# A RetNet and gated-MLP step on one core: the gate's activations in halves, a low part on another engine, and two edits in the retention loop

## The chip, the core and the metric

The kernel runs on one core of a Trainium2 chip, as one program. A core has five engines that work through queues of their own and wait for each other by semaphores: TensorE (PE) for matrix products and transposes, VectorE (DVE) and ScalarE (ACT) for work on tiles, GpSimd (POOL) for tiles and some transfers, and SyncE (SP), which here only issues transfers. Operands lie in the on-chip memory SBUF, products of PE arrive in eight banks of PSUM. The metric is the time of one execution on the device in microseconds.

## What is computed

Two layers over a prompt of 1024 tokens and 8 single new tokens ("decode"), width 1024, all in fp32. The first layer mixes tokens by retention (4 heads, keys of 256, values of 512), the second by a gated MLP whose spatial mixing works on chunks of 128 tokens. The parts of the reference that the change touches:

```python
# retention: o is the retention's output of a head, normalised over its 512 values
mu = jnp.mean(o, -1, keepdims=True)
var = jnp.mean(jnp.square(o - mu), -1, keepdims=True)
o = ((o - mu) * lax.rsqrt(var + LN_EPS)).reshape(B, L, RET_VW) * gn_gain
y = (jax.nn.silu(g) * o) @ w_out
...
# gated MLP
u, v, g = jnp.split(x @ w_in, 3, axis=-1)
u = jax.nn.gelu(u, approximate=False)
v = _layer_norm(jax.nn.gelu(v, approximate=False), ln_g, ln_b)
mixed = jnp.einsum('gij,bcjgd->bcigd', ws, vc) + b_s      # vc: v in chunks of 128 tokens, 8 groups of 256
y = u * mixed * jax.nn.silu(g)
return y @ w_out, v
```

Each layer ends with x = LayerNorm(ALPHA * x + mixer(x)).

## The kernel before

**Products.** An fp32 operand is held as two tiles: a high part `h`, the rounding to a shorter format (fp32r), and a low part `l`, the rest. `mm3` (line 65) makes each product of three matmuls, h·h, h·l and l·h. So whatever goes into PE has to be split first: a copy that rounds (on ACT), and a subtraction for the rest (on DVE or POOL). Some low parts are made in another way: ACT writes -t, rounded, into the low tile (line 1346 for `vl`), and a transfer that POOL issues adds t to it (line 1347), which leaves the rest.

**What sets the order.** The program runs under a manual schedule: every engine executes its instructions in the order in which the Python code emits them. A list `later` collects functions; `run_later` emits what stands in it at the start of the next step. Tiles come from a pool of 49 equal slots, whose reuse makes the writer of a new tile wait for the last reader of the old one; products come in 8 banks of PSUM.

**Retention's chunk loop** (about 581 to 762 us of the span). 16 steps n, four chunks of 256 tokens for each of four heads. In step n the code emits: the statistics of chunk n-1's output (`r_stat`: DVE, then a power on POOL that gives `rs`); for chunk n+1 the transposes of the key `kt`, the split of what was loaded (ACT, then POOL: `qkl`, `vl`), the normalised output of chunk n-1 (`r_on`: `nb` on DVE, then `on` on ACT, line 605) and the scores `sc`; then for chunk n the state update `st`, the inner product and the cross product with the state into `o` (both PE), and the transposes `y` of the normalised chunk n-1 (line 619), which DVE multiplies by the gate into `yT`. The cross product doesn't exist in the first chunk of a head (n%4 = 0).

**The gate stage** (about 1135 to 1540 us). 16 units, two for each of the 8 groups of 256 columns of v; unit n has the tiles fm(40+n). A unit makes 128 columns of u and of s (the gate) at once, with seven products by Strassen-Winograd, in the order p5, p1, p3, p6, p2, p7 and, after the next unit's p5, p4. Each has two steps of 12 matmuls of 258 columns, for the two pieces `c` of half of the tokens. p1, p6, p7 and p4 add up in the same PSUM bank (`fm..a`), p5 and p3 in another (`fm..c`), p2 in a third. After p5, p1 and p3 ACT copies the bank into the tile u or s (line 1189), after p6, p2 and p7 DVE adds it to them (line 1193); p4 ends as a gelu straight from the bank (line 1191). So p6 must wait until ACT has copied, and p7 and p4 until DVE has added. The first half of u, made before, gets its gelu later (line 1200), s its silu (line 1197 in units of odd n, line 1202 in even ones), and then DVE multiplies u and s (line 1203). Beside this, group by group, `s_prep` normalises v (DVE, tiles `lv`) and splits it into `vh` and `vl` and the mixing weight into `wsh` and `wsl`, `s_mix` mixes (PE `mx`, then ACT), and `s_y` transposes the result (PE `yt`, line 1371) and multiplies it by u (DVE `yy`). The weights of the next units are loaded, combined and split in pieces (`wr`, `wt`, `w_p`) in between.

Of the kernel before, what the change touches and what calls it, by code (L numbers as in the profile page):

```python
# [13 lines left out]
AF = mybir.ActivationFunctionType  # L14
ALU = mybir.AluOpType
# [6 lines left out]
T = SEQ + NB  # L22
# [5 lines left out]
NCH = SEQ // CH  # L28
# [6 lines left out]
HT = T // 2  # L35
# [6 lines left out]
def retnet_gmlp_step(ctx: ExitStack, tc: tile.TileContext, a, o):  # L42
    nc = tc.nc
    act, dve, pool, pe, sp = nc.scalar, nc.vector, nc.gpsimd, nc.tensor, nc.sync
# [8 lines left out]
    def S(name, shape=(128, T), dt=F32):  # L53
        return big.tile(list(shape), dt, tag="s", name=name)

    def PS(name):
        return psp.tile([128, 512], F32, tag="ps", name=name)

    def f(ap):
        return ap.bitcast(F32)  # L60
# [4 lines left out]
    def mm3(out, lh, ll, rh, rl, start, stop, skip=False):  # L65
        mm(out, lh, rh, start, False, skip)
        mm(out, lh, rl, False, False, skip)
        mm(out, ll, rh, False, stop, skip)
# [43 lines left out]
    def wload(p):  # L112
        if p >= NP:
            return
        for half in range(2):
            wload_half(p, half)
# [22 lines left out]
    later = []  # L139

    def run_later():
        todo, later[:] = later[:], []
        for fn in todo:
            fn()
# [319 lines left out]
    def dec_gate():  # L464
        dve.tensor_tensor(ydT, ydT, gd, ALU.mult)
        dve.tensor_copy(yd[:, :, 0:8], ydT)
        dve.tensor_tensor(yd[:, :, 8:16], ydT, f(yd[:, :, 0:8]), ALU.subtract)
# [30 lines left out]
    def r_pre(n):  # L498
        if n >= NS:
            r_on(n - 2)  # L500
            return
        r = R[n]
        ps = PS(f"kt{n}")
        for jb in range(2):
            for d in range(2):
                pe.transpose(ps[:, jb * 256 + d * 128:jb * 256 + (d + 1) * 128],
                             r["qk"][:, 2 + d, jb * 128:(jb + 1) * 128], ident)
        kd = S(f"kd{n}", (128, 2, 512), F32R)
        act.copy(kd[:, 0, :], ps)
        dve.tensor_tensor(kd[:, 1, :], ps, f(kd[:, 0, :]), ALU.subtract)  # L510
        r["kd"] = kd
        if n:
            r_split(n + 1)
        r_on(n - 2)
        sc = PS(f"sc{n}")
        hh, ll = r["qkh"], r["qkl"]
        for jb in range(2):
            for d in range(2):
                ks = slice((2 + d) * CH + jb * 128, (2 + d) * CH + (jb + 1) * 128)
                qs = slice(d * CH + jb * 128, (d + 1) * CH)  # L520
                mm3(sc[:, jb * CH:CH + jb * 128], hh[:, ks], ll[:, ks], hh[:, qs], ll[:, qs], d == 0, d == 1)
        pt = S(f"p{n}", (128, 384))
        dve.tensor_tensor(pt, sc[:, :384], RC["mask"], ALU.mult)
        phl = S(f"phl{n}", (128, 2, 384), F32R)
        act.copy(phl[:, 0, :], pt)
        pool.tensor_tensor(phl[:, 1, :], pt, f(phl[:, 0, :]), ALU.subtract)
        r["p"] = phl
# [45 lines left out]
    def r_cross(n):  # L573
        r = R[n]
        if n % NCH == 0:
            return
        sh, sl = r["s"]
        for ib in range(2):
            for d in range(2):
                qs = slice(d * CH + ib * 128, d * CH + (ib + 1) * 128)  # L580
                mm3(r["o"][ib], r["qkh"][:, qs], r["qkl"][:, qs], sh[:, d, :], sl[:, d, :], False, d == 1)

    def r_stat(n):
        if n < 0:
            return
        h, c = divmod(n, NCH)
        r = R[n]
        st = small.tile([128, 2, 6], F32, tag="st", bufs=4, name=f"st{n}")
        mv = small.tile([128, 2, 2], F32, tag="mv", bufs=3, name=f"mv{n}")
        for ib in range(2):  # L590
            dve.bn_stats(st[:, ib, :], r["o"][ib])
        for ib in range(2):
            dve.bn_aggr(mv[:, ib, :], st[:, ib, :])
        r["mv"], r["rs"] = mv, rstd_of(mv[:, :, 1], epsg[:, 2 * h:2 * h + 2], 128, 2, f"n{n}")

    def r_on(n):
        if n < 0:
            return
        r = R[n]
        rs = r["rs"]  # L600
        nb = small.tile([128, 2], F32, tag="nb", name=f"nb{n}")
        dve.scalar_tensor_tensor(nb, r["mv"][:, :, 0], -1.0, rs[:, 0:2], ALU.mult, ALU.mult)
        on = S(f"on{n}", (128, 2, DV))
        for ib in range(2):
            act.activation(on[:, ib, :], r["o"][ib], AF.Identity, bias=nb[:, ib:ib + 1], scale=rs[:, ib:ib + 1])
        r["on"] = on
# [188 lines left out]
    def x_op(key, kt, sl):  # L795

        hh, ll = X[key]
        return hh[kt // 2][:, kt % 2, sl], ll[kt // 2][:, kt % 2, sl]
# [134 lines left out]
    for n in range(NS):  # L933
        run_later()
        if n == 4:
            dec_gate()
        r_stat(n - 1)
        r_pre(n + 1)
        r_state(n)
        r_inner(n)  # L940
        if n % NCH == 1:
            r_cross(n)
        r_y(n - 1)
        if n % NCH != 1:
            r_cross(n)
        r_load(n + 3)
        if n == NS - 5:
            wload(24)
        if n == NS - 4:
            wload(25)  # L950
        if n >= NS - 4:
            wsplit(24, n - NS + 4, eng=pool)
        if n == NS - 1:
            for t2 in range(4):
                outb.ysplit(0, t2)
            outb.pre_load(0)
            outb.pre_load(1)
# [176 lines left out]
    class FmUnit(Unit):  # L1134
# [38 lines left out]
        def step(self, k, c):  # L1173
            ch, first = BANK[k], k in self.FIRST
            if first:
                self.ps[ch, c] = PS(f"fm{self.p}{ch}_{c}")
            ps = self.ps[ch, c][:, :258]
            wh, wl = self.op[k]
            sl = slice(c * 258, c * 258 + 258)
            for kt in range(4):  # L1180
                ws = slice(kt * 128, kt * 128 + 128)
                mm3(ps, wh[:, ws], wl[:, ws], *x_op(XKEY[k], kt, sl), first and kt == 0, kt == 3, skip=not first)
            i, n = OUT[k]
            if k == "p5":
                if c == 0:
                    self.q = [S(f"{s}{self.n}") for s in "us"]
            t = self.q[n][:, i * HT + c * 258:i * HT + c * 258 + 258]
            if k in ("p5", "p1", "p3"):
                act.copy(t, ps)
            elif k == "p4":  # L1190
                act.activation(t, ps, AF.Gelu)
            else:
                dve.tensor_tensor(t, t, ps, ALU.add)
            if c == 1:
                u, s = self.q
                if k == "p7" and self.n % 2:
                    later.append(lambda: act.activation(s, s, AF.Silu))
                if k == "p4":
                    def out():
                        act.activation(u[:, :HT], u[:, :HT], AF.Gelu)  # L1200
                        if self.n % 2 == 0:
                            act.activation(s, s, AF.Silu)
                        later.append(lambda: dve.tensor_tensor(u, u, s, ALU.mult))
                    later.append(out)

    X1_SUMS = {}
    for n, (key, part) in {10: ("s1", 0), 11: ("s1", 3), 13: ("s1", 2), 14: ("s1", 5), 15: ("s2", 0), 16: ("s2", 3),
# [23 lines left out]
    first, at, n = {}, {}, 16  # L1231
# [90 lines left out]
    def s_prep(g, part):  # L1322

        if g >= GR:
            return
        q = G[g]
        if part == 0:
            wr = q["wr"]
            pool.affine_select(out=wr, in_=wr, pattern=[[1, 128]], compare_op=ALU.is_ge, fill=0.0, base=0,
                               channel_multiplier=-1)  # L1330
            wh = small.tile([128, 128], F32R, tag="wsh", name=f"wsh{g}")
            wl = small.tile([128, 128], F32R, tag="wsl", name=f"wsl{g}")
            act.copy(wh, wr)
            dve.tensor_tensor(wl, wr, f(wh), ALU.subtract)
            q["w"] = (wh, wl)
            q["vhl"] = []
        half, k = divmod(part, 4)
        t = q["v"][half]
        tb = half * 4 + k
        dve.scalar_tensor_tensor(t[:, k, :], t[:, k, :], vmv[:, tb, 0:1], q["gt"], ALU.subtract, ALU.mult)  # L1340
        dve.scalar_tensor_tensor(t[:, k, :], t[:, k, :], vrs[:, tb:tb + 1], q["bt"], ALU.mult, ALU.add)
        if k == 3:
            hh = S(f"vh{g}_{half}", (128, 4, 256), F32R)
            ll = S(f"vl{g}_{half}", (128, 4, 256), F32R)
            act.copy(hh, t)
            act.mul(ll, t, -1.0)
            pool.dma_start(ll, t, accum_op=ALU.add)
            q["vhl"].append((hh, ll))

    def s_mix(g):  # L1350
# [102 lines left out]
    for u, k in seq:  # L1453
        for i in range(u.STEPS):
            s = first[u, k] + i
# [95 lines left out]
```

## Time and profile before

| | |
|---|---|
| time, median of 3 runs | 1748.51 us (1746.86 to 1751.27) |
| the profiled execution | 1749.73 us, its span 1748.0 us |
| PE busy | 1692.2 us, 97% of the span |
| DVE busy | 900.0 us, 51% |
| ACT busy | 664.9 us, 38% |
| POOL busy | 407.5 us, 23% |
| granted clock of PE over the span | 0.987 of full speed |

The busy shares are means over stages with different limits. PE's idle time is where another engine sets the pace, and the view of waits tells which; the granted clock is what the throttle gave PE in a stretch, as a share of 2.4 GHz. The profile numbers the units' tiles (fm41a is bank a of the unit with n = 1), but not the chunks: `y` or `on` stand for all.

### The profile page before, as it was taken

How to read it: one execution, taken by the hardware profiler on the slowest of the kernel's cores; microseconds unless marked ns; L12 is line 12 of the kernel's file. 1: busy time of each engine (PE TensorE's matmuls, PEld its weight loads, DVE VectorE, ACT ScalarE, POOL GpSimd, SP SyncE). 2: the span in 40 equal slices, each digit the busy share in tenths (PEclk: the TensorE clock that was granted, in tenths of full speed). 3: DMA queues.
4: the chain of work that ended last, by engine and by line, in shares of the span. 5: the costliest groups of instructions: out<-in, count | busy, mean ns of one | idle time of the engine just before them, and what ended most of it. 6: DMA issues, size and time to landing. Idle time of an engine off the chain costs nothing. (4 is left out here: it accounts for less than half of the span.)

```text
span 1748.0 us, 25438 instructions
## 1 busy us (share of the span) xinstructions
PE 1692.2 (97%) x10304; PEld 1511.5 (86%) x10304; DVE 900.0 (51%) x1446; ACT 664.9 (38%) x1043; POOL 407.5 (23%) x331
## 2 busy tenths in 40 slices
PE   9999999999999999999999999997899999999996
PEld 8898897979999887877778999996889999977775
DVE  7134453633331577753359574564465555543347
ACT  4122424234332454431205343344556666731102
POOL 4122231411110666531107100011111111231103
PEclk9999999999999999999999999998999999999998
DMA  7135555555532544341102312263655666692206
GB/s 266 72 122 191 183 204 187 212 165 209 217 145 93 197 157 157 133 181 49 49 25 110 110 73 97 84 178 78 152 147 151 157 164 157 152 324 89 82 1 171
DMA packets 103174, 248.76 MB, mean 142 GB/s; under 512 B 9264, under 2 KB 37824, under 8 KB 103056
## 3 DMA queue, kind: packets, MB, share of 16 engines
q1 hardware_dynamic: 92736, 222.78, 36.5%
q0 software_dynamic: 10112, 24.15, 7.8%
q8 instruction: 81, 1.33, 0.3%
q14 instruction: 37, 0.30, 0.0%
q10 hardware_dynamic: 208, 0.20, 0.0%
HBM read 152.83 MB, written 69.93 MB: 127 GB/s over the span
## 5 line engine op out<-in xcount | busy, mean ns | idle before, releaser
L63 PE MATMUL fm<-xl,wh 128*128 128x344 f32 x768 | 246.6, 321 | 1.2 <-DVE xl L301 0.8
L63 PE MATMUL fm<-xh,wh 128*128 128x344 f32 x768 | 246.4, 321 | 1.3 <-ACT xh L300 1.3
L63 PE MATMUL fm<-xh,wl 128*128 128x344 f32 x768 | 246.1, 320 | 0.0
L63 PE MATMUL op<-wh,yh 128*128 128x512 f32 x512 | 202.4, 395 | 0.0
L63 PE MATMUL op<-wl,yh 128*128 128x512 f32 x512 | 201.7, 394 | 0.0
L63 PE MATMUL op<-wh,yl 128*128 128x512 f32 x512 | 201.7, 394 | 0.0
L63 PEld LDWEIGHTS fm<-xh,wh 128*128 128x128 f32 x768 | 144.9, 189 | 5.6 <-ACT xh L300 2.0
L63 PEld LDWEIGHTS fm<-xl,wh 128*128 128x128 f32 x768 | 144.7, 188 | 3.0 <-DVE xl L301 1.3
L63 PEld LDWEIGHTS fm<-xh,wl 128*128 128x128 f32 x768 | 144.7, 188 | 0.0
L130 ACT CAST wh<-wr 128x1024 fp32r<-128x1024 f32 x83 | 86.0, 1047 | 143.0 <-PE pd L63 58.9
L665 DVE TENSOR_TENSOR pre<-pre,op 128x512 f32<-128x512 f32 x96 | 65.7, 684 | 141.4 <-PE op L63 141.4
L134 DVE TENSOR_TENSOR wl<-wr,wh 128x1024 fp32r<-128x1024 f32 x77 | 107.6, 1403 | 46.2 <-ACT wh L130 28.6
L412 DVE SCALAR_TENSOR_TENSOR dw<-s,qd_dec,dw 128x512 f32<-128x512 f32 x32 | 40.0, 1251 | 170.1 <-ACT dw L411 170.1
L63 PEld LDWEIGHTS op<-wh,yh 128*128 128x128 f32 x512 | 96.1, 188 | 23.8
L63 PEld LDWEIGHTS op<-wh,yl 128*128 128x128 f32 x512 | 96.1, 188 | 22.7
L63 PEld LDWEIGHTS op<-wl,yh 128*128 128x128 f32 x512 | 96.2, 188 | 22.2
L63 PE MATMUL tm<-wl,xh 128*128 128x512 f32 x256 | 101.1, 395 | 0.0
L63 PE MATMUL tm<-wh,xl 128*128 128x512 f32 x256 | 100.9, 394 | 0.0
L63 PE MATMUL tm<-wh,xh 128*128 128x512 f32 x256 | 100.9, 394 | 0.0
L420 POOL TENSOR_TENSOR dhl<-dw,dhl 128x512 fp32r<-128x512 f32 x32 | 43.3, 1353 | 242.3 <-ACT dhl L419 234.4
L355 ACT ACTIVATE v<-tm,gneg 128x512 f32<-128x512 f32 x32 | 22.0, 689 | 202.3 <-PE tm L63 184.6
L1171 POOL DMA_DIRECT2D w_p<-wr x32 | 28.6, 895 | 295.8 <-PE tm38a L63 169.6
(829 smaller groups left out, 4262.4 us busy)
## 6 DMA issues: line engine op xcount, KB each, us to landing
wr<-in_w SPq DMA_DIRECT2D x127, 512.0 KB
s<-in_state SPq DMA_DIRECT2D x32, 512.0 KB
out_rs<-s SPq DMA_DIRECT2D x32, 512.0 KB
y_s<-yy SPq DMA_DIRECT2D x17, 512.0 KB
qk_s<-ro SPq DMA_DIRECT2D x16, 512.0 KB
v_s<-v SPq DMA_DIRECT2D x16, 512.0 KB
vbc<-vd_s SPq DMA_DIRECT2D x16, 512.0 KB
g_s<-g SPq DMA_DIRECT2D x16, 512.0 KB
```

What stands on the lines that cost most here:

```text
L63: pe.matmul(out, lhs, rhs, start=start, stop=stop, skip_group_check=skip)
L130: act.copy(t, src)
L134: eng.tensor_tensor(t, src, f(W[p][half][0]), ALU.subtract)
L355: act.activation(t[:, i % 2, :], ps, AF.Copy, scale=gneg[:, 2 * h + i % 2:2 * h + i % 2 + 1])
L412: dve.scalar_tensor_tensor(w[:, 0, :], s[:, 0, :], qd_dec[:, h, 0, b:b + 1], w[:, 1, :], ALU.mult, ALU.add)
L420: pool.tensor_tensor(hl[:, 1, :], w, f(hl[:, 0, :]), ALU.subtract)
L665: dve.tensor_tensor(dst, dst, ps, ALU.add)
L1171: pool.dma_start(self.op[k][1], src, accum_op=ALU.add)
```

## The change

Four edits. In retention, `nb` = -mean x rs, one instruction over two columns with two tensor inputs, becomes two instructions over one column, each with one tensor and rs as a scalar operand. The cross product of chunk n is emitted ahead of the transposes of chunk n-1 in all steps; before, only where n%4 was 1. In the gate, silu is cut in two halves of the columns, and the pieces (gelu, silu, silu, product) are emitted one for each step of the schedule in place of together. And `vl` is no longer made by an ACT multiplication and an adding transfer, but by a DVE subtraction that is emitted one step after `vh`.

```diff
         nb = small.tile([128, 2], F32, tag="nb", name=f"nb{n}")
-        dve.scalar_tensor_tensor(nb, r["mv"][:, :, 0], -1.0, rs[:, 0:2], ALU.mult, ALU.mult)
+        for ib in range(2):
+            dve.tensor_scalar(nb[:, ib:ib + 1], r["mv"][:, ib, 0:1], -1.0, rs[:, ib:ib + 1], ALU.mult, ALU.mult)
...
         r_inner(n)
-        if n % NCH == 1:
-            r_cross(n)
+        r_cross(n)
         r_y(n - 1)
-        if n % NCH != 1:
-            r_cross(n)
         r_load(n + 3)
...
                 u, s = self.q
+                lo, hi = slice(0, HT), slice(HT, T)
+                todo = []
                 if k == "p7" and self.n % 2:
-                    later.append(lambda: act.activation(s, s, AF.Silu))
+                    todo = [lambda: act.activation(s[:, lo], s[:, lo], AF.Silu),
+                            lambda: act.activation(s[:, hi], s[:, hi], AF.Silu)]
                 if k == "p4":
-                    def out():
-                        act.activation(u[:, :HT], u[:, :HT], AF.Gelu)
-                        if self.n % 2 == 0:
-                            act.activation(s, s, AF.Silu)
-                        later.append(lambda: dve.tensor_tensor(u, u, s, ALU.mult))
-                    later.append(out)
+                    todo = [lambda: act.activation(u[:, lo], u[:, lo], AF.Gelu)]
+                    if self.n % 2 == 0:
+                        todo += [lambda: act.activation(s[:, lo], s[:, lo], AF.Silu),
+                                 lambda: act.activation(s[:, hi], s[:, hi], AF.Silu)]
+                    todo.append(lambda: dve.tensor_tensor(u, u, s, ALU.mult))
+
+                def chain():
+                    if todo:
+                        todo.pop(0)()
+                        later.append(chain)
+                later.append(chain)
...
             act.copy(hh, t)
-            act.mul(ll, t, -1.0)
-            pool.dma_start(ll, t, accum_op=ALU.add)
+            later.append(lambda: dve.tensor_tensor(ll, t, f(hh), ALU.subtract))
             q["vhl"].append((hh, ll))
```

How the order of the engines moves, at three places. The rows name line, operation and out<-in; a number right behind a name is the chunk, group or unit. The lines of the changed kernel are numbered by its own code.

PE in step n = 6 of the retention loop, where the inner product of chunk 6 (o6 from vh6, vl6) is followed by the transposes of chunk 5 and the cross product of chunk 6 (o6 from sh5, sl5). Before:

```order
L63 MATMUL o6_1_5545<-vl6_5281,phl6_5406 128x512
L63 MATMUL o6_1_5545<-vh6_5280,phl6_5406 128x512
L619 MATMUL y5_0_5556<-ident_71,on5_5502 128x128 x4
L619 MATMUL y5_1_5563<-ident_71,on5_5502 128x128 x4
L63 MATMUL o6_0_5544<-sh5_5426,qkh6_5276 128x512
L63 MATMUL o6_0_5544<-sl5_5427,qkh6_5276 128x512
```

Now, from the last cross products on:

```order
L63 MATMUL o6_1_5551<-sh5_5431,qkh6_5279 128x512
L63 MATMUL o6_1_5551<-sl5_5432,qkh6_5279 128x512
L63 MATMUL o6_1_5551<-sh5_5431,qkl6_5280 128x512
L620 MATMUL y5_0_5574<-ident_71,on5_5508 128x128 x4
L620 MATMUL y5_1_5581<-ident_71,on5_5508 128x128 x4
L506 MATMUL kt8_5604<-ident_71,qk8_5473 128x128 x4
```

The two groups of four transposes moved behind all 12 matmuls of the cross product, up to the transposes `kt` of the next step.

ACT between unit 10 (tiles fm50, u10, s10) and unit 11 (fm51), behind unit 10's last product. Before:

```order
L1191 ACTIVATE u10_12867<-fm50a_0_12918 128x258
L1191 ACTIVATE u10_12867<-fm50a_1_12933 128x258
L1200 ACTIVATE u10_12867<-u10_12867 128x516
L1202 ACT_TABLE_LOAD
L1202 ACTIVATE s10_12868<-s10_12868 128x1032
L1333 CAST wsh6_13200<-gbw6_13112 128x128
L1189 COPY u11_13129<-fm51a_0_13206 128x258
L1189 COPY u11_13129<-fm51a_1_13221 128x258
```

Now:

```order
L1189 ACTIVATE u10_12881<-fm50a_0_12933 128x258
L1189 ACTIVATE u10_12881<-fm50a_1_12948 128x258
L1200 ACTIVATE u10_12881<-u10_12881 128x516
L1339 CAST wsh6_13213<-gbw6_13126 128x128
L1187 COPY u11_13143<-fm51a_0_13219 128x258
L1202 ACT_TABLE_LOAD
L1202 ACTIVATE s10_12882<-s10_12882 128x516
L1187 COPY u11_13143<-fm51a_1_13234 128x258
L1203 ACTIVATE s10_12882<-s10_12882 128x516
```

The copy of the mixing weight `wsh6` moved from behind the silu to ahead of the table load, and the two copies of unit 11's bank now stand ahead of and between the two halves of the silu.

DVE in unit 11, from the last normalisation of the first half of group 6's v (lv6_0) on. Before:

```order
L1341 SCALAR_TENSOR_TENSOR lv6_0_13108<-lv6_0_13108,vrs_105,gbw6_13112 128x256
L1193 TENSOR_TENSOR u11_13129<-u11_13129,fm51b_0_13332 128x258
L1036 TENSOR_TENSOR w52_p1_13323<-wr52_0_13071,w52_p1_13323 128x512
L1193 TENSOR_TENSOR u11_13129<-u11_13129,fm51b_1_13347 128x258
L1193 TENSOR_TENSOR s11_13130<-s11_13130,fm51a_0_13206 128x258
L1193 TENSOR_TENSOR s11_13130<-s11_13130,fm51a_1_13221 128x258
```

Now:

```order
L1347 SCALAR_TENSOR_TENSOR lv6_0_13122<-lv6_0_13122,vrs_105,gbw6_13126 128x256
L1191 TENSOR_TENSOR u11_13143<-u11_13143,fm51b_0_13345 128x258
L1352 TENSOR_TENSOR vl6_0_13343<-lv6_0_13122,vh6_0_13342 128x1024
L1034 TENSOR_TENSOR w52_p1_13338<-wr52_0_13085,w52_p1_13338 128x512
L1191 TENSOR_TENSOR u11_13143<-u11_13143,fm51b_1_13361 128x258
L1191 TENSOR_TENSOR s11_13144<-s11_13144,fm51a_0_13219 128x258
L1191 TENSOR_TENSOR s11_13144<-s11_13144,fm51a_1_13234 128x258
```

The subtraction for vl6_0, which reads ACT's vh6_0, stands ahead of a weight piece, the second add into u11 and the adds into s11 of product p7.

## Rows read from the trace of the kernel before

**Rows 1.** Waits of PE, by releaser: us in total, times, longest us.

```profile
PE y L619 <- ACT on L605: 10.3, 12, 2.4
PE mx L63 <- DMA vl<-lv: 7.9, 2, 4.7
PE yt L1371 <- ACT u L1191: 3.9, 2, 3.1
...
PE fm44c L63 <- ACT s L1189: 2.3, 1, 2.3
PE fm41a L63 <- ACT u L1189: 2.0, 1, 2.0
...
PE fm43a L63 <- DVE s L1193: 1.2, 1, 1.2
```

**Rows 2.** Busy us by stretch: length, engines, PE clock, DMA share, GB/s.

```profile
600.00:700.00 100.00, 91.30 (x488) 75.94 (x487) 77.03 (x139) 49.62 (x66) 61.79 (x38) 0.97 0.44 145
1150.00:1300.00 150.00, 128.94 (x935) 122.48 (x936) 77.21 (x162) 75.28 (x137) 21.11 (x26) 0.92 0.52 125
1300.00:1510.00 210.00, 208.55 (x1696) 205.92 (x1695) 133.08 (x279) 131.54 (x238) 35.04 (x43) 1.00 0.63 158
```

**Rows 3.** The instructions of line 602: duration ns min/median/max, first and last start.

```profile
L602 DVE SCALAR_TENSOR_TENSOR nb<-mv,rsrn x16: 160/2331/2391, 596.6 to 757.9; 128x2 f32<-128x2 f32 x16
```

**Rows 4.** Timeline around chunk 1's `on`: start us, us, instruction, [idle before, releaser].

```profile
604.07 0.40 PE L63 MATMUL st<-vl,kd 128*128 128x512 f32 x1
...
604.30 0.63 PE L63 MATMUL st<-vh,kd 128*128 128x512 f32 x2
...
607.28 2.38 POOL L495 TENSOR_TENSOR qkl<-qk,qkh 128x1024 fp32r<-128x1024 f32 x1
...
607.34 2.33 DVE L602 SCALAR_TENSOR_TENSOR nb<-mv,rsrn 128x2 f32<-128x2 f32 x1 [0.20 <-POOL rsrn L254]
...
610.60 0.33 PE L619 MATMUL y<-ident,on 128*128 128x128 f32 x1 [2.42 <-ACT on L605]
```

**Rows 5.** Timeline of POOL and DVE at two later places of the span.

```profile
939.28 2.39 POOL L713 TENSOR_TENSOR pred<-pred,lnb 8x1024 f32<-8x1024 f32 x1
...
939.77 0.15 DVE L251 TENSOR_SCALAR rstl<-lmv 128x1 f32<-128x1 f32 x1
...
1526.53 4.78 POOL L134 TENSOR_TENSOR wl<-wr,wh 128x1024 fp32r<-128x1024 f32 x2 [11.02 <-ACT wh L130]
...
1529.01 2.33 DVE L1380 CAST y1d<-ydt 128x8 fp32r<-128x8 f32 x1
```

**Rows 6.** The tile vl: time from a transfer's issue to its landing.

```profile
DMA to landing us min/median/max: 4.5/6.1/8.8
```

**Rows 7.** DVE's subtraction of 128x1024 on line 1036: duration ns min/median/max.

```profile
L1036 DVE TENSOR_TENSOR wl_p<-wt,wh_p x6: 1218/1222/1227, 1010.8 to 1121.1; 128x1024 fp32r<-128x1024 f32 x6
```

**Rows 8.** Timeline of ACT in the gate stage, units 41 and 44.

```profile
1212.57 1.06 ACT L1346 ACTIVATE vl<-lv 128x1024 fp32r<-128x1024 f32 x1 [0.64 <-DMA w_p<-wt]
...
1266.73 0.62 ACT L1164 CAST w_p<-wr 128x512 fp32r<-128x512 f32 x1 [5.22 <-DMA vl<-lv]
```

**Rows 9.** Timeline of ACT, DVE and PE in unit 51.

```profile
1443.93 1.05 ACT L1345 CAST vh<-lv 128x1024 fp32r<-128x1024 f32 x1 [0.96 <-PE fm51a L63]
...
1444.10 0.68 DVE L1036 TENSOR_TENSOR w_p<-wr,w_p 128x512 fp32r<-128x512 f32 x1
...
1445.04 0.75 DVE L1193 TENSOR_TENSOR s<-s,fm51a 128x258 f32<-128x258 f32 x2
...
1447.92 0.28 PE L63 MATMUL fm51a<-x1h,w_p 128*128 128x258 f32 x1
```

**Rows 10.** Timeline of ACT and DVE between units 50 and 51.

```profile
1430.56 1.28 ACT L1202 ACT_TABLE_LOAD   x1
...
1432.83 0.28 ACT L1333 CAST wsh<-gbw 128x128 fp32r<-128x128 f32 x1
...
1433.14 0.29 DVE L1334 TENSOR_TENSOR wsl<-gbw,wsh 128x128 fp32r<-128x128 f32 x1 [9.55 <-ACT wsh L1333]
```

## The prediction

> **What bounds the kernel now.** TensorE (PE) is busy nearly throughout, as the table of the profile says, and the change leaves its matmuls and transposes as they are. So it can win only PE's idle time and the time that PE runs at a lower clock. The first view is who waited for whom on PE [rows 1]: the reader is to see that the largest waits stand in the two stages that the change touches. In the chunk loop of retention the transposes `y` wait 10.3 us for `on`, in 12 places. In the gate stage `mx` waits 7.9 us for the transfer that makes `vl`, `yt` 3.9 us for a gelu, fm44c 2.3, fm41a 2.0 and fm43a 1.2 us for copies and adds on ScalarE (ACT) and VectorE (DVE). The second view, busy time and granted clock by stretch [rows 2], adds what waits cost behind themselves. From 600 to 700 PE is idle for 8.7 us and its granted clock averages 0.97 of 2.4 GHz; from 1150 to 1300 it is idle for 21.1 us at 0.92; from 1300 to 1510 it is idle for 1.5 us at 1.00. Busy time at a lower clock loses the missing share: 0.03 x 91.3 = 2.7 us in the loop, 0.08 x 128.9 = 10.3 us in the gate. So one us of wait costs (8.7 + 2.7) / 8.7 = 1.31 us in retention and (21.1 + 10.3) / 21.1 = 1.49 us in the gate's first part. With 10.3 x 1.31 = 13.5 us in retention and 31.4 in the gate, 45 us is all there is to win; the forecast is what part of it goes.
>
> **Retention, the mean term.** `nb` takes between 160 and 2391 ns, with a median of 2331 [rows 3]. The timeline shows why: one starts at 607.34 and ends at 609.67, just when the subtraction for `qkl` on GpSimd (POOL, 607.28 to 609.66) ends; ACT's `on` has to wait for it, and PE has idled 2.42 us for `on` at 610.60 [rows 4]. This DVE instruction with two tensors from SBUF stands still beside POOL's. The change replaces it with two instructions of one column that read one tensor each. The trace has such a one: `rstl`, one column, one tensor, took 0.15 us at 939.77 although a sum on POOL ran from 939.28 to 941.67. It also has a row against it: the cast of `y1d`, 8 columns and one tensor, took 2.33 us from 1529.01, and ended at 1531.34, just when two subtractions on POOL, one after the other from 1526.53, ended at 1531.31 [rows 5]. So the bounds for the pair are 0.30 and about 2.4 us. I take 0.30, because `rstl` is the same operation in the same shape. The Trainium skill ("SBUF — State Buffer", section "Who interferes with whom") says that a VectorE instruction with one SBUF input keeps clear of GpSimd outside the two-port modes, but that a tensor_scalar can enter such a mode and then contends. The `y1d` row agrees with the second half, the `rstl` row with the first; by the second half alone, rival (a) below would come out.
>
> **Retention, the order.** In the iterations with n%4 of 2 and 3 (8 of 16), the 12 matmuls of the cross product now stand ahead of the 8 transposes of y; with n%4 = 1 they did already, with n%4 = 0 there is no cross product. Matmuls of this width follow each other by 0.23 us (604.07 and 604.30 [rows 4]), so `on` gets 12 x 0.23 = 2.8 us more, and the longest wait for it was 2.4 [rows 1]. No transfer moves with it. The price: DVE's statistics of the next chunk now stand behind its evacuation of the later y, so `nb` and `on` of that chunk come later against PE. Where the next iteration has a cross product, that hides it; in n = 4, 8 and 12 nothing does, and I allow 0.15 us each at 1.31, which with rounding is 0.5 us. So of the 13.5 us **13.0** go. The two edits cover each other: for all but the chunks in front of n = 4, 8 and 12 either would do.
>
> **Gate, the low part of v.** It was an ACT multiplication, a DMA issued by POOL, and a landing 4.5 to 8.8 us after the issue, with 6.1 as the median [rows 6]. Now DVE subtracts, 128x1024 from two SBUF tensors: 1.22 us by `wl_p`, the same form [rows 7]. ACT loses 16 x 1.06 us [rows 8], POOL 16 issues, DVE gains 16 x 1.22 = 19.5 us. In the steady part DVE is busy for 133.1 of 210 us [rows 2], so the sum has room; the question is only what stands behind it. The two `mx` waits go, since the subtraction takes the place of a multiplication and of at least 4.5 us to the landing: 7.9 x 1.49 = **11.8**. The fm44c wait goes too: ACT's cast at 1266.73 had idled for 5.22 us until a `vl` transfer landed, and the copy that PE waited for stood behind it [rows 8]. I take **3.0** of 2.3 x 1.49 = 3.4.
>
> A new wait comes with it: the subtraction waits for ACT's vh, and queued behind it on DVE are a weight piece and the adds into u and s, for which PE's next product waits. In unit 51 vh ran from 1443.93 to 1444.98; a weight piece and an add began at 1444.10 and took until the s adds at 1445.04, of which two last 0.75 us; and PE began the product p4, which needs the first, at 1447.92 [rows 9]. With the subtraction in front, the first s add ends at 1444.98 + 1.22 + 0.94 + 0.38 = 1447.52 (half of the two adds), 0.40 us before PE needs it. So it costs nothing there, but only just. At the gate's start (units 40 to 44) the slots of the pool come free in another order, and I expect DVE to hold up a copy for product p6 of unit 41 in place of ACT: **-2.0** there, an estimate that takes fm41a's 2.0 us once more. Bounds: +3.0 if fm41a's wait goes (2.0 x 1.49), -7.2 if four of the first five units wait the 1.2 us of a subtraction.
>
> **Gate, halves.** The silu over 1032 columns becomes two pieces; the gelu stays one piece of 516, and a step of the schedule lies between pieces. The number of table loads stays. ACT's `wsh` came at 1432.83, behind the table load that began at 1430.56 and the whole silu; DVE's queue idled for 9.55 us until it, and began at 1433.14 [rows 10]. Now `wsh` stands right behind the gelu, where the load stood: 1432.83 - 1430.56 = 2.27 us earlier, and the whole run of DVE's work behind it too. That removes fm43a's wait, 1.2 x 1.49 = **1.8**; in the steady part there is no PE wait to remove. For `yt`, the multiplication of 1.06 us and the 0.64 us idle ahead of it, between the two gelus [rows 8], leave the path: 1.7 x 1.49 = **2.5**; vh stays between them, and with it the rest of that wait. The product u*s of even units (about the 1.22 us of [rows 7]) moves from ahead of two weight pieces to right ahead of the yy product that reads it. That costs nothing while the 2.27 us earlier start hides the wait for the second silu half; without it, 1.2 us in each even unit's successor.
>
> **The sum.** 13.0 + 11.8 + 3.0 + 1.8 + 2.5 - 2.0 = 30.1 us. The profiled execution took 1749.7 us, 1.7 more than its span, and the median of the three runs was 1748.5. The profiled execution is 1.2 us off that median, so the terms are taken over unscaled: 1748.5 - 30.1 = **1718 us**.
>
> **Rivals.** (a) *The pair waits for POOL like the old instruction.* For it: the `y1d` cast; against it: `rstl` [rows 5]. The reordering still covers the chunks that are followed by a cross product, but the three y in n = 4, 8 and 12, whose statistics come later into POOL's run, pay 2.2 us each: 3 x 2.2 x 1.31 = 8.6, which gives 1727. (b) *The gate's start trades one wait for another.* DVE waits for vh, a slot or the decode rows ahead of the adds in units 41 to 45; the lower bound comes, 5.2 us worse, and yt's 2.5 stay: 1726. (c) *DVE's queue becomes the bound*, slower than before. If vh comes later than now, each odd unit's s adds come later by as much. Up to 0.40 us that is free; at 4 us the eight odd units pay 8 x 3.60 x 1.49 = 43 us, which gives 1761. For it: that margin. Against it: ACT has 16 x 1.06 us less to do. It crosses the old time at about 30.1 / (8 x 1.49) + 0.40 = 2.9 us of lateness. (d) *The waits only change owner* in both stages, and PE waits as long for another releaser: 1747.
>
> **How the numbers follow.** The forecast has 0.70, (a) 0.10, (b) 0.13, (c) 0.04, (d) 0.03. The forecast's own spread is 1709 to 1725: below, 3.0 in place of -2.0 and the rest of `yt` (2.2 x 1.49 = 3.3); above, half of the mx gain lost. The range goes on to 1732 over (a) and (b) and what they share, and down to 1706 for small waits that I left out. Faster by over 0.3% (about 5 us, what a measurement of this kernel can tell from no change) holds the forecast, (a) and (b): 0.93; within it (d): 0.03; slower (c): 0.04.
>
> **What would show it.** In the changed kernel's trace: 32 instructions of `nb` near 0.15 us with POOL running beside them; no `y` wait above 0.4 us, and a clock of 1.00 from 600 to 700; no wait of `mx`; a DVE `vl` of 1.22 us; `wsh` ahead of the table load and DVE's run some 2.3 us earlier; units 45 to 54 without PE waits. It would be wrong if `nb` still takes 2.3 us, if products p4 or p7 of odd units wait for s adds, or if units 41 to 43 still show several us of waits.

## The result, and the profile after

| | before | after |
|---|---|---|
| median | 1748.34 us (4 runs) | 1729.13 us (4 runs, 1728.48 to 1731.05) |
| ratio | | 0.989, 95% interval 0.9873 to 0.9907 |
| profiled execution, its span | 1749.73, 1748.0 us | 1728.71, 1726.9 us |

The kernel became faster by 19.2 us, 1.1%. The forecast was 30.1 us less, 1718; the time lies inside the range of 1706 to 1732, near its upper end. The direction and most of the mechanisms held, and a third of the forecast gain is missing. The rest of this document is about that third.

The view of PE's waits of the changed kernel, with the columns of [rows 1]:

```profile
PE fm41c L63 <- ACT s L1187: 4.4, 2, 3.9
PE fm42a L63 <- DVE s L1191: 3.0, 2, 2.4
PE fm41a L63 <- ACT u L1187: 3.0, 1, 3.0
PE op L63 <- DVE yl L643: 2.9, 1, 2.9
PE yt L1376 <- ACT u L1189: 2.8, 2, 1.5
PE fm41a L63 <- DVE s L1191: 2.7, 1, 2.7
...
PE fm55a L63 <- DVE s L1191: 1.5, 1, 1.5
...
PE y L620 <- ACT on L606: 0.7, 2, 0.3
...
PE fm43a L63 <- DVE s L1191: 0.6, 1, 0.6
```

Against [rows 1], the 10.3 us of `y` became 0.7, `mx` and fm44c no longer wait for a transfer or a copy, fm43a's wait halved. New at the top are three waits of unit 41, one of unit 42 and one of `op`, the first product behind the retention loop. Busy time and clock by stretch, to be laid beside [rows 2] (the gate's stretches begin 11 us earlier here, as the gate does):

```profile
600.00:700.00 100.00, 99.29 (x556) 84.57 (x555) 77.17 (x163) 53.52 (x70) 73.95 (x42) 1.00 0.44 147
1139.00:1289.00 150.00, 131.76 (x996) 126.71 (x997) 92.94 (x185) 73.36 (x143) 16.68 (x21) 0.94 0.41 109
1289.00:1500.00 211.00, 211.00 (x1713) 208.35 (x1713) 137.80 (x273) 126.59 (x242) 26.22 (x33) 1.00 0.53 139
```

In the loop PE is now idle for 0.7 of 100 us at a full clock, in place of 8.7 at 0.97. In the gate's first part it is still idle for 18.2 us, where it was 21.1: that is where the forecast's gain is missing.

Where the time went is read from when a tile's first matmul starts (the number behind the min/median/max). Before, then after:

```profile
L63 PE MATMUL op<-wh,yh x512: 387/394/482, 751.6 to 1733.8; 128*128 128x512 f32 x171
...
L63 PE MATMUL fm40c<-xs1h,w_p x16: 278/284/289, 1135.3 to 1138.1; 128*128 128x258 f32 x16
L63 PE MATMUL fm42c<-xs1h,w_p x16: 277/416/419, 1195.0 to 1199.3; 128*128 128x258 f32 x16
L63 PE MATMUL fm46c<-xs1h,w_p x16: 278/283/289, 1310.1 to 1312.8; 128*128 128x258 f32 x16
```

```profile
L63 PE MATMUL op<-wh,yh x512: 387/394/484, 736.7 to 1712.5; 128*128 128x512 f32 x171
...
L63 PE MATMUL fm40c<-xs1h,w_p x16: 278/282/287, 1124.0 to 1126.7; 128*128 128x258 f32 x16
L63 PE MATMUL fm42c<-xs1h,w_p x16: 277/282/286, 1188.4 to 1191.2; 128*128 128x258 f32 x16
L63 PE MATMUL fm46c<-xs1h,w_p x16: 277/282/293, 1290.0 to 1292.8; 128*128 128x258 f32 x16
```

The out-projection of retention (`op`) begins 14.9 us earlier; at the gate's begin (fm40c), behind the new wait of `op`, 11.3 of that are left. From there to unit 42 the changed kernel *loses* 4.7 us (6.6 left at fm42c), although the first wait of mx, 4.7 us, lay in that stretch and is gone; from unit 42 to unit 46 it wins 13.5 (20.1 at fm46c). Behind that little changes: the span ends 21.1 us earlier. (Both profiled executions stand within 1.5 us of their medians, so this differs a little from 19.2.)

More than half of what was won from unit 42 to 46 is clock, not waits. PE's busy time and granted clock from fm40c to fm42c and from there to fm46c (stretch, length, PE busy, clock, DMA share, GB/s), before, then after:

```profile
1135.30:1195.00 59.70, 51.17 (x383) 0.94 0.65 164
1195.00:1310.10 115.10, 100.99 (x746) 0.93 0.50 125
```

```profile
1124.00:1188.40 64.40, 53.76 (x382) 0.87 0.47 122
1188.40:1290.00 101.60, 93.49 (x745) 1.00 0.46 127
```

From fm40c to fm42c PE's idle time grew from 8.5 to 10.6 us, and its busy time by 2.6 us at a lower clock. From fm42c to fm46c the idle time fell from 14.1 to 8.1 us and the busy time by 7.5, because the clock was 1.00 in place of 0.93.

### The profile page after: what moved, and what is told of

Read it like the earlier page. It is cut to its first block, busy times and chain, and to the rows that moved or that the text cites. A ratio compares the mean times of both kernels' runs of the same rounds, so it can differ in the third digit from the quotient of the medians.

```text
span 1726.9 us, 25389 instructions
## 1 busy us (share of the span) xinstructions
PE 1682.3 (97%) x10304; PEld 1507.2 (87%) x10304; DVE 907.9 (53%) x1478; ACT 655.4 (38%) x1045; POOL 399.0 (23%) x315
```

## The experiments

**The four parts alone.** First, only the mean term:

```diff
-        dve.scalar_tensor_tensor(nb, r["mv"][:, :, 0], -1.0, rs[:, 0:2], ALU.mult, ALU.mult)
+        for ib in range(2):
+            dve.tensor_scalar(nb[:, ib:ib + 1], r["mv"][:, ib, 0:1], -1.0, rs[:, ib:ib + 1], ALU.mult, ALU.mult)
```

> Only the mean term: two one-column instructions in place of one. Theory: either retention edit alone covers most of the waits of the transposes. nb then takes about 0.21 us each of two beside GpSimd as in the changed kernel, on comes 1.9 us earlier in the nine chunks that had a slow nb, so the four long waits of y (1.3 to 2.4 us) shrink under 0.5 us, 10.3 us of waits become 3 and the time falls by 9 to 12 us, to about 1738. Rival: the order is what did it, and the time falls by less than 4 us.

Measured: 1736.06 us against 1748.92, ratio 0.9924 (0.9906 to 0.9942), 12.9 us less. The instructions of nb in this kernel (ns min/median/max), and its wait of y:

```profile
L603 DVE TENSOR_SCALAR nb<-mv,rsrn x32: 203/210/220, 596.3 to 744.9; 128x1 f32<-128x1 f32 x32
...
PE y L620 <- ACT on L606: 1.5, 5, 0.3
```

None of the 32 is over 0.22 us, though a POOL subtraction ran beside 22 of them, where nine of the 16 old ones stood near 2.35 beside POOL. That settles the mean term: it alone brings what I had forecast for both retention edits (13.0), and a little more than the 9 to 12 us expected of it here.

Second, only the order:

```diff
-        if n % NCH == 1:
-            r_cross(n)
+        r_cross(n)
         r_y(n - 1)
-        if n % NCH != 1:
-            r_cross(n)
```

> Only the order: the cross product ahead of the transposes in all steps, nb as before. Theory: the chunks that are followed by a cross product are covered, as with the mean term alone (9 us less), but some of the three transposes in steps 4, 8 and 12 get a slow nb, 2.2 us each with nothing to cover it, so the fall is 4 to 9 us, to about 1742. Rival: the order does everything by itself, 13 us less; then the mean term is worth nothing.

Measured: 1751.64 us, ratio 1.0014 (1.0004 to 1.0024), 2.7 us *more*, where I had expected 4 to 9 less. The other eight waits of y are 0.34 us or less, so the cover works for PE there; but `op` waits 0.9 and 0.8 us, which it did not before, and the three waits in steps 4, 8 and 12 came (2.45, 2.29 and 2.91 us). My reason for those was wrong. The timeline of this kernel around step 4, all engines:

```profile
618.03 2.35 DVE L602 SCALAR_TENSOR_TENSOR nb<-mv,rsrn 128x2 f32<-128x2 f32 x1 [0.27 <-POOL rsrn L254]
...
620.41 1.45 ACT L605 ACTIVATE on<-o,nb,rsrn 128x512 f32<-128x512 f32 x2 [5.29 <-DVE nb L602]
...
622.16 1.07 ACT L559 ACTIVATE so<-T 128x1024 f32<-128x1024 f32 x1
...
623.25 0.40 SPq L560 DMA_DIRECT2D out_rp<-so  x1
623.75 0.53 SPq L482 DMA_DIRECT2D qk<-qk_s  x1
...
627.43 0.16 DVE L602 SCALAR_TENSOR_TENSOR nb<-mv,rsrn 128x2 f32<-128x2 f32 x1 [0.27 <-POOL rsrn L254]
...
628.41 1.05 ACT L494 CAST qkh<-qk 128x1024 fp32r<-128x1024 f32 x1 [4.45 <-DMA qk<-qk_s]
...
631.21 1.44 ACT L605 ACTIVATE on<-o,nb,rsrn 128x512 f32<-128x512 f32 x2
...
632.03 0.33 PE L619 MATMUL y<-ident,on 128*128 128x128 f32 x1 [2.45 <-ACT on L605]
```

The nb of the chunk that waits (627.43) is short. It is the one *before* it that is slow (618.03): it holds up `on`, behind which ACT makes the head's state `so`, for which the store `out_rp` waits in SP's queue, and behind the store the loads of a later chunk. ACT idles 4.45 us for that load, and `on` stands behind the split of what is loaded. So PE, ahead by what the order won, meets loads that come no earlier. A further kernel tested this: as the one just shown, with the store emitted a step later, behind the loads:

```diff
-            sp.dma_start(o["rp"][h].rearrange("(d p) e -> p d e", p=128), so)
+            later.append(lambda: sp.dma_start(o["rp"][h].rearrange("(d p) e -> p d e", p=128), so))
```

> As e2_order (the cross product first, nb as before), and the store of a head's state (out_rp from so) is emitted one step later, behind the three loads of the chunk that is fetched three steps ahead. Theory: in e2_order the y of steps 4, 8 and 12 waited because SyncE's queue held the loads of qk behind that store, which waits for so, which ACT executes behind the on that a slow nb holds up; with the store behind the loads, ACT no longer idles 4 to 5 us for qk there, the waits of 2.4, 2.3 and 2.9 us shrink below 1 us, and the time falls by 6 to 10 us against e2_order, to about 1743. Rival: the loads wait for their own slots or for the memory, and come no earlier: 1751.

Measured: 1742.22 us, ratio 0.996 (0.9945 to 0.9975), 9.4 us below the order alone. What ACT idled for `qk` on line 494 (us, times), with the order alone and then with the store moved, and the remaining wait of y in the second:

```profile
  DMA qk<-qk_s: 17.4, 5
```

```profile
  DMA qk<-qk_s: 2.6, 2
...
PE y L619 <- ACT on L605: 4.9, 15, 1.1
```

With the store behind the loads, most of ACT's idle time for `qk` is gone, and so are the long waits of y. That shows the chain: a slow nb holds up ACT, ACT the store, and the store the loads behind it in SP's queue. The nb of step 4 is now itself slow, as the prediction had feared (2.34 us at 627.52), but y waits only 1.07 us there.

Third, only the halves (the part of the diff in `step` that builds `todo` and `chain`):

```diff
-                    later.append(lambda: act.activation(s, s, AF.Silu))
+                    todo = [lambda: act.activation(s[:, lo], s[:, lo], AF.Silu),
+                            lambda: act.activation(s[:, hi], s[:, hi], AF.Silu)]
...
-                    def out():
...
+                    todo = [lambda: act.activation(u[:, lo], u[:, lo], AF.Gelu)]
...
+                    todo.append(lambda: dve.tensor_tensor(u, u, s, ALU.mult))
```

> Only the halves of silu and their spread over steps; the low part of v as before. Theory: the mixing weight's copy comes 2.3 us earlier, the waits of fm43a and fm45a (2.6 us) go, the two waits of mx for the transfer stay, so 2 to 5 us less, about 1745. Rival: the pieces shift the slots of the pool and cost at the gate's start what the changed kernel lost there in unit 41 (7 us of waits, some 10 in time), so 5 us more than before, about 1753.

Measured: 1751.01 us, ratio 1.0009 (0.9998 to 1.002): no difference that can be told. Both theories missed. fm43a no longer waits (1.2 us before), and `mx` waits 6.3 us in place of 7.9, but fm45a's wait stayed (1.6 us), and the trace has new waits for s adds (fm41a 2.7 us where the kernel before had 1.1 in all, fm53a 1.6 where there was none).

Fourth, only the low part of v:

```diff
-            act.mul(ll, t, -1.0)
-            pool.dma_start(ll, t, accum_op=ALU.add)
+            later.append(lambda: dve.tensor_tensor(ll, t, f(hh), ALU.subtract))
```

> Only the low part of v by a VectorE subtraction. Theory: the mx waits and fm44c's go (15 us), and the subtraction, which waits for the slot of a weight piece that product p3 of unit 41 reads, holds up the decode rows and the copies behind them there: waits of 4, 3 and 3 us at fm41c and fm41a, which cost 10 us; so 5 us less, about 1743. Rival: the hold-up in unit 41 comes from the halves, and this part alone gives the 15 us, about 1733.

Measured: 1738.63 us, ratio 0.9941 (0.9921 to 0.9962), 10.3 us less, between the theory's 5 and the rival's 15. Its waits of PE show what it costs:

```profile
PE fm41c L63 <- ACT s L1189: 4.4, 2, 3.8
PE fm41a L63 <- ACT u L1189: 3.0, 1, 3.0
```

So this part, and not the halves, makes these two waits of unit 41. The four differences add up to -12.9 + 2.7 + 2.1 - 10.3 = -18.4 us, near the -19.2 of all four together.

**Parts taken back from the changed kernel.** The old order of the loop in an otherwise changed kernel:

```diff
-        r_cross(n)
+        if n % NCH == 1:
+            r_cross(n)
         r_y(n - 1)
+        if n % NCH != 1:
+            r_cross(n)
```

> The changed kernel with the retention loop's old order; the other three parts stay. Theory: with the short nb the order saves only some waits of 0.1 to 0.3 us, 1.2 us in all, and costs 3 us at the loop's end, where the first product of the out-projection waits 2.9 us for a subtraction on VectorE that stands beside GpSimd's. Undoing it gives 2 us, to about 1727. Rival: the order is worth its part of what I forecast, and undoing it costs 2 us or more, 1731.

Measured: 1726.42 us, ratio 0.9864 (0.985 to 0.9879), 2.7 below the changed kernel. The interval still touches that of the changed kernel, so the size is not sharp; but op no longer waits in its trace. The old order in the last step alone:

```diff
-        r_cross(n)
+        if n < NS - 1:
+            r_cross(n)
         r_y(n - 1)
+        if n == NS - 1:
+            r_cross(n)
```

> The changed kernel with the old order in the last step of the retention loop alone (transposes of chunk 14 ahead of the cross product of chunk 15). Theory: there the later transposes make VectorE's first subtraction for the out-projection start behind GpSimd's, where it stands still; with the old order in this step alone the wait of 2.9 us at op goes and the time falls by 2 to 4 us, to about 1726. Rival: the wait has to do with the short nb, not the order, and stays: 1729.

Measured: 1726.52 us, ratio 0.9867 (0.9853 to 0.9882), the same again. DVE's and POOL's timeline at the loop's end, in the changed kernel (with PE's wait) and then with the old last step:

```profile
736.76 5.74 POOL L643 TENSOR_TENSOR yl<-yT,yh 128x1024 fp32r<-128x1024 f32 x2 [2.25 <-ACT yh L642]
...
738.12 5.46 DVE L643 TENSOR_TENSOR yl<-yT,yh 128x1024 fp32r<-128x1024 f32 x2
...
740.31 0.50 PE L63 MATMUL op<-wh,yl 128*128 128x512 f32 x1 [2.90 <-DVE yl L643]
```

```profile
736.17 1.22 DVE L643 TENSOR_TENSOR yl<-yT,yh 128x1024 fp32r<-128x1024 f32 x1
...
736.87 6.16 POOL L643 TENSOR_TENSOR yl<-yT,yh 128x1024 fp32r<-128x1024 f32 x2 [2.28 <-ACT yh L642]
```

The subtraction yl for the out-projection has two tensors from SBUF. Behind the later transposes DVE begins its first at 738.12, when POOL has been at its own for 1.4 us, and stands still for a while; with the old last step it begins 0.7 us ahead of POOL's and takes 1.22 us.

The silu in one piece in an otherwise changed kernel (the old lines of `step`, as in the diff above, with plus and minus exchanged):

> The changed kernel with silu in one piece and emitted as before; the other three parts stay. Theory: the halves put the product of u and s of even units among the adds that p7 waits for, which cost 1.6 us more in unit 41 and 1.4 more in unit 42, and save 0.7 in unit 43 and 0.5 in unit 55; undoing them gives 2 to 3 us, to about 1726.5. Rival: they give the 1.8 us forecast, and undoing costs that, 1731.

Measured: 1730.95 us, ratio 0.9891 (0.9876 to 0.9907), against 0.989 (0.9873 to 0.9907) with the halves: not told apart. In its trace the s waits of fm41a fall from 2.7 to 1.0 us, as I had expected, but that of fm42a only from 3.0 to 2.8, and those of fm43a and fm55a rise from 0.6 to 1.3 and from 1.5 to 2.0. The halves shift waits; neither my +1.8 nor the loss that I then expected is shown.

**The gate's start.** The changed kernel's timeline in unit 41, ACT, DVE and PE:

```profile
1161.63 1.04 ACT L1351 CAST vh<-lv 128x1024 fp32r<-128x1024 f32 x1 [3.72 <-issue]
1162.58 0.37 ACT L1187 COPY s<-fm41c 128x258 f32<-128x258 f32 x1
...
1163.00 0.58 PE L63 MATMUL fm41c<-xs4h,w_p 128*128 128x258 f32 x1 [3.85 <-ACT s L1187]
...
1166.04 1.22 DVE L1352 TENSOR_TENSOR vl<-lv,vh 128x1024 fp32r<-128x1024 f32 x1 [12.60 <-PE fm41c L63]
1167.18 1.27 DVE L1293 SCALAR_TENSOR_TENSOR vd<-vd,vdmv,vdg 8x1024 f32<-8x1024 f32 x1
...
1168.48 0.38 ACT L1187 COPY u<-fm41a 128x258 f32<-128x258 f32 x1 [4.45 <-DVE vd L1293]
...
1168.91 0.58 PE L63 MATMUL fm41a<-xs2h,w_p 128*128 128x258 f32 x1 [2.96 <-ACT u L1187]
```

DVE's queue stands for 12.60 us at the first vl. It does not wait for vh, which is there at 1162.67, but until PE ends product p3 (fm41c), which makes nothing that vl reads: it is the last reader of the tile in whose slot vl is put (w41_p3, weights of p3). PE for its part ran p3 late, because the copy of s stands on ACT behind vh, and vh had waited for its slot (the profile names no releaser; in the program the slot held wt41_1, which is read by a transfer that POOL issued at 1158.21 and that landed 3.3 us later). Behind vl on DVE is vd, the normalisation of the decode rows; the copy of u waits for vd, because it takes the slot of what vd reads (vdg0). So p6 waits too. The next kernel takes vd out of that queue by emitting it two steps earlier:

```diff
-        if (fb, o) in ((1, 2), (4, 2)):
+        if (fb, o) in ((1, 0), (4, 2)):
             vd_norm(fb // 4)
```

> The changed kernel with the normalisation of the decode rows (vd) emitted two steps earlier, ahead of the subtraction for the first vl in place of behind it. Theory: the waits of 3.9 us at fm41c and 3.0 at fm41a come from slots of the pool that are let go too late because the subtraction holds up the queue of VectorE; with vd ahead, the subtraction's slot and that of vh come free by the end of p1, the two waits shrink to under 2 us together, and the time falls by 5 to 9 us, to about 1722. Rival: the vd rows must wait for their own loads there, the waits only move, and the time stays at 1729.

Measured: 1718.7 us, ratio 0.9821 (0.9804 to 0.9837), 10.4 below the changed kernel. That is a little more than expected. Both waits are gone from the view of waits; vl on DVE and the gate's first part (the columns of [rows 2]):

```profile
1159.53 1.23 DVE L1352 TENSOR_TENSOR vl<-lv,vh 128x1024 fp32r<-128x1024 f32 x1 [1.12 <-ACT vh L1351]
...
1139.00:1289.00 150.00, 139.65 (x1089) 134.99 (x1088) 102.07 (x208) 81.25 (x158) 18.49 (x23) 0.98 0.46 124
```

vl now waits 1.12 us, for vh. PE's idle time there falls from 18.2 to 10.4 us and its clock rises from 0.94 to 0.98. In the program the edit does two things: it takes vd out of the queue behind vl, and, since vd's tiles come free earlier, it deals out the slots anew. The first vl now stands in the slot of w41_p1, whose last reader is the earlier product p1, and vh in that of vd itself. That fits the slots as the cause; the two effects, and the single slots, were not tried apart.

**Better versions.** Both repairs together, the early decode rows and the old last step:

> The changed kernel with both repairs: the decode rows normalised two steps earlier, and the old order in the last step of the retention loop. Theory: the two lie in different stages and add up, 10.4 + 2.6 us less than the changed kernel's 1729.1, so 1716. Rival: they share something (the out-projection's start moves what arrives at the gate's start), and the sum is 1718 to 1719.

Measured: 1714.34 us, ratio 0.9807 (0.9794 to 0.9821): the lowest median here. At 14.8 us below the changed kernel, the two add up or a little more. Last, the same with vh a step later, to take it from between the gelus that yt waits for:

```diff
-            act.copy(hh, t)
-            later.append(lambda: dve.tensor_tensor(ll, t, f(hh), ALU.subtract))
+            def split():
+                act.copy(hh, t)
+                later.append(lambda: dve.tensor_tensor(ll, t, f(hh), ALU.subtract))
+            later.append(split)
```

> As f1_both, and the copy vh is emitted one step later, so that it no longer stands between the two gelus that the yt transposes of unit 41 wait for. Theory: the second wait of yt shrinks from 1.5 to under 0.5 us, which is worth 1.5 us, so 1714.5; the subtraction, one more step behind, still comes before mx. Rival: vh comes later, so DVE's queue waits longer for it ahead of the s adds, and units 42 and later wait for those: 1718 or more.

Measured: 1716.18 us, ratio 0.9813 (0.98 to 0.9826), not told apart from the last one. Its waits show the exchange: yt's second wait is gone, and unit 42's wait for s, 1.6 us in the kernel with both repairs, more than doubled.

```profile
PE fm42a L63 <- DVE s L1194: 3.5, 1, 3.5
...
PE yt L1382 <- ACT u L1192: 1.3, 1, 1.3
```

```profile
1188.56 1.29 DVE L1385 TENSOR_TENSOR yy<-yt,u 128x512 f32<-128x512 f32 x2 [9.58 <-DMA w_p<-wt]
```

The later vh is not what holds up the adds: vl has no wait in this run of DVE's work. The run begins with yy, behind a transfer, and goes on with hardly a stop to the s add that PE waits for, at 1198.69, some 10 us later. In the kernel with both repairs it is as long (1189.33 to 1199.46; there it begins with vl, which had waited for vh). So a PE that comes earlier to unit 42 only waits longer. DVE's queue is the bound there, as in rival (c) of the prediction, but not for the reason (c) gives.

## Why the prediction held, and where it missed

**What bounds the kernel** was right: nearly all that was won was PE's idle time and clock in the two stages, and the part behind unit 46 gave only 1.0 us. The price of 1.31 to 1.49 us for each us of wait held as a mean over the gate's first part: in the changed kernel 18.2 us of idle time stand beside 0.06 x 131.8 = 7.9 us lost to the clock, a price of 1.43, and with the early decode rows 10.4 beside 2.8, a price of 1.27. It is not the price of a single wait. From fm42c to fm46c the changed kernel was idle for 8.1 us at a clock of 1.00. And behind the same 2.9 us of `op`, the clock was 1.00 in the changed kernel (741 to 744) and 0.50, the lower level of 1.2 GHz, in the one with the early rows (740.95 to 744.20).

By the starts of the tiles, retention and what follows it up to the gate won 11.3 us of the 13.0 forecast, and the gate up to unit 46 won 8.8 (20.1 less 11.3) of 17.1. So most of what is missing lies in the gate.

**The mean term** was right in mechanism and size: 0.21 us for each of 32, and 0.33 for a pair, whose second begins before the first has ended, against the 0.30 taken from `rstl`; the loop won 14.1 us up to `op` (14.9 less the 0.8 by which it began earlier), 13.0 with the mean term alone. Rival (a) is refuted by the row of nb above. The Trainium skill ("SBUF — State Buffer", section "Who interferes with whom") says that a tensor_scalar can enter a two-port mode, and then contend with GpSimd, where its operands meet that mode's conditions. The 0.20 to 0.22 us of nb beside POOL show no such contention for one column. The same section of the Trainium skill says that a VectorE instruction with two SBUF inputs contends with a GpSimd instruction that reads SBUF. The `yl` rows above agree (2.13 us for the first behind POOL's, 1.22 ahead of it).

**The order** was sized too well. Three things failed. "Either would do" for all but three chunks: alone, the order lost 2.7 us, since the slow nb acts through the store and the loads as well, which I had not followed. "No transfer moves with it": true of the emission, but the queue of SP waits for ACT, and that I had left out. And the price at the loop's end was missing: I priced the later transposes only by the next step's nb and on, and the last step has no next one; behind it stand the subtractions for the out-projection, beside POOL. That was 2.9 us of wait, some 2.6 in time.

**The low part of v** brought in sum what was forecast where it should, but in part by luck. mx's 7.9 us and fm44c's 2.3 are gone, and from unit 42 to 46 the kernel won 13.5 us; the forecast's terms for that stretch are the second mx wait (3.2 x 1.49 = 4.8), 3.0, 1.8 and 2.5, together 12.1. The items differ. The 1.4 us of fm45a, which also went, I had left out, and fm42a waits 2.4 us longer for s. PE's idle time fell by only 6.0 us in all; the other 7.5 are clock, where the price of 1.49 would give 2.9. The tight place in unit 51 held: no unit from 45 to 54 waits.

**The term that was mis-sized is the gate's start**, -2.0 with a lower bound of -7.2. From fm40c to fm42c the kernel lost 4.7 us net of the first mx wait. With that wait at its bare 4.7 us, the price was 9.4 us; at the forecast's 4.7 x 1.49 = 7.0 it was 11.7. It lies between, since a part of the clock that the old wait cost fell behind fm42c, whose matmuls took 416 ns before and take 282 now. The end of the chain, which I had named (DVE holds up a copy for p6 of unit 41), was there and cost 2.96 us of wait. What I did not see was its start: that vl's slot hangs on p3, and that vh waits for a slot too, with the copy of s behind it on ACT (3.85 us); and u*s in the run of adds made p7's wait 2.7 in place of 1.1. My bound assumed that each unit would at most wait for one subtraction of 1.2 us; the queue waited 12.60 us for a slot. This one term explains 7.4 to 9.7 of the 10.9 us between forecast and result, and `op` some 2.6. Taking back `op`'s wait and two of unit 41's three gave 1714.

**The halves** were forecast at 1.8 + part of the yt term. wsh did come earlier and fm43a's wait halved, but runs with and without them can't be told apart. The sentence "That costs nothing while the 2.27 us earlier start hides the wait" failed in unit 41, where DVE's queue did not start earlier, since it stood at vl.

**Rivals and range.** (b), the gate's start, came true and at more than its price: 9.4 to 11.7 us, where it took 7.2. Against that, yt gained 1.1 of 3.9 us of wait, where the forecast took 1.7 and (b) none. The time, 1729, is nearer to (b)'s 1726 than to the forecast; it lies in the range because the range was drawn over the rivals. (c) didn't decide; its mechanism, a vl that waits for vh ahead of the adds, appears in unit 42, an even one, with 2.4 us at fm42a. The spread of 1709 to 1725 is a microsecond wider on each side than its terms give: 1718.4 - 5.0 - 3.3 = 1710 and 1718.4 + 5.9 = 1724.

**The signs.** Of the three that the prediction named for being wrong, the nb of 2.3 us did not come. The other two did: p7 of unit 41 waited 2.7 us for s adds where it had waited 1.1 (p7 of unit 55, 1.5 where it had 2.0), and units 41 and 42 show several us of waits.

## What to carry to other kernels

When an edit gives an engine a new instruction, write down what its *output tile's slot* waits for, not only its inputs: in a queue that runs in order, one late slot holds up everything behind it, and the bound is when the slot's last reader ends, not the instruction's length. When instructions are moved in a loop, price the last step by itself, since what follows it is not the next step. And if a short instruction sits between two engines' queues, as nb did, a cover on PE does not replace making it short: its delay went on through a store and the loads behind it. A price for a us of wait that is read from a stretch is a mean; a single wait can cost itself alone, or the lower clock behind it as well.

## What the runs showed of the hardware

A DVE tensor_scalar of one column with its second scalar in SBUF took 0.20 to 0.22 us in all 32 places; in the changed kernel a POOL subtraction ran beside 26 of them. The form with one constant took 0.15 us [rows 5]. A one-input cast of 8 columns had stood still beside POOL for 2.33 us [rows 5], so the number of tensors alone doesn't decide; whether it is the one column or the operation was not tried.

For two-input instructions the order of issue decided who stood still. DVE's first `yl` took 1.22 us when it began 0.7 us ahead of POOL's, and two of them took 5.46 us when POOL had begun first. The old nb shows it too: the nine that began 0.07 to 0.10 us behind a POOL subtraction took 2.33 to 2.39 us, and two that began 0.07 and 0.12 us ahead of one took 0.16. One of those two, in the kernel before:

```profile
618.65 0.16 DVE L602 SCALAR_TENSOR_TENSOR nb<-mv,rsrn 128x2 f32<-128x2 f32 x1 [0.23 <-POOL rsrn L254]
...
618.72 2.40 POOL L495 TENSOR_TENSOR qkl<-qk,qkh 128x1024 fp32r<-128x1024 f32 x1
```

So emitting the old nb a little ahead of POOL's subtraction might have done the same as the one-column form; no run tried it.
